# Neighbourhood attention: high and low parts of the probabilities side by side in one product with the values

## The chip, the cores and the metric

The kernel runs on one core of a Trainium2 chip. A core has a matrix engine (TensorE, PE in the profile, with its weight loads as PEld), a vector engine (VectorE, DVE), a scalar engine (ScalarE, ACT), a general engine (GpSimd, POOL) and a queue engine for transfers (SyncE, SP). The metric is the device time of one execution in microseconds; the kernel before takes 2171.08 us, the median of 3 runs (2170.97 to 2171.12).

## The reference

One encoder layer in float32 is applied to two inputs, a sample of 512 tokens and a prompt of 1024 tokens, each of width 1024. Cut to what matters:

```python
z = rmsnorm(x) @ w_in      # q_A k_A v_A | q_B k_B v_B | gate_A gate_B
o_a = attention over all tokens (8 query heads, 2 key heads, rotary)
o_b = neighbourhood_attention(q_B, k_B, v_B, rpb)
x = x + (sigmoid(gate_A) * (o_a @ w_pa) + sigmoid(gate_B) * (o_b @ w_pb)) @ w_out
x = x + relu(rmsnorm(x) @ w_up)**2 @ w_down
y = rmsnorm(x)
```

Neighbourhood attention is what the change touches. Tokens lie on a grid 64 columns wide. A query sees a window of 8 rows by 16 columns around itself; per head (8 heads of 64)

```python
s = einsum('bqhd,bkhd->bhqk', q, k) * scale + bias        # bias by row and column offset
s = where(mask, s, -1e30);  p = softmax(s)
o = einsum('bhqk,bkhd->bqhd', p, v)
```

## The kernel before

**Precision.** Matrix products of float32 quality are made from operands rounded to float32r. A value x is cut into a high part, `hi = round(x)`, written by ScalarE (a copy into a float32r tile), and a low part, `lo = x - hi`, written by VectorE (a subtraction). Most products are then three: hi·hi, hi·lo and lo·hi (`mm3`, L195 to L197).

**Stages.** The work runs in this order: branch A of the sample, branch B of the sample, its projections and output; the same for the prompt; then the MLP of both. In the profile branch B lies at about 190 to 322 us (sample) and 806 to 1090 us (prompt).

**Branch B.** It works in units of one head and one strip of 16 grid columns, 8 x 4 = 32 units per input. A strip has 128 queries in the sample (8 rows) and 256 in the prompt (16 rows, two halves of 128). Each half looks at a rectangle of keys 32 columns wide: 256 keys in the sample, 384 in the prompt. A unit has three steps, each lagging a unit or two behind the one before:

- `s_unit`: scores on TensorE (L933, tiles sbs), bias and row maximum on VectorE (L936), exponential and row sum on ScalarE (L941), reciprocal on VectorE (L943), scaling on GpSimd (L944, tile pbs).
- `t_unit`: the probabilities are transposed by TensorE in blocks of 128 x 128 (L956, tiles ptbs in PSUM); ScalarE writes the high parts (L961, tile bhs), VectorE the low parts (L962, tile bls). The two tiles are laid out as (128 keys) x (key block) x (half) x (128 queries).
- `v_unit`: products with the values into one PSUM bank (L977, tile obs). The values of a key block, tile vss, are the stationary operand, 128 keys x 128 columns: 64 columns of high parts and 64 columns of low parts. The moving operand is the high tile, then the low tile, of the same key block, accumulated into the same bank. The sample has two key blocks, each 128 queries wide: four products of 128 columns. The prompt has four key blocks, of which two are seen by both halves (256 columns) and two by one half (128 columns): four products of 256 columns and four of 128.

The output bank then holds, on partitions 0 to 63, p·v_hi and, on partitions 64 to 127, p·v_lo, for p = p_hi + p_lo. `finish_o` adds them: ScalarE copies the upper half to a tile ot (L430), VectorE adds the lower half to it into a tile os (L439, or L434 for the last two heads). For the first six heads os goes to DRAM (tensor obd) by a transfer issued from ScalarE's queue (L440); for the last two heads it is cut into high and low parts on the chip (L435, L436; tile oXs). Branch A uses the same `finish_o` with 512 queries (tiles os, ot_As, os_As).

**What fills TensorE meanwhile.** While a unit's softmax runs on the other engines, TensorE works off products that belong to no unit: the gate's (tiles gpss), and towards the end the projection of branch A (tiles ppas). They are generators of which a set number of steps is pulled between the steps of a unit. The queries and keys of the next pair of heads are also projected in between, once every eight units (tiles pqbs, pkbs; evacuated at L877 to L903).

**Buffers.** Gate, projection, transposes and outputs of branch B take turns in one pool of four PSUM banks (`mm`); scores have a pool of their own. Tile ot has one buffer, os two, bhs and bls two each.

**Order.** Each engine works off its own queue strictly in order. The order in a queue is set by the framework's planner, which starts from the program's order and moves instructions by estimated times, except where the program pins them (`keep_in_program_order`, not used here). Waits between engines are semaphores set by the framework from what reads and writes which tile.

Of the kernel before, what the change touches and what calls it, by code (L numbers as in the profile page):

```python
# [12 lines left out]
F32R = mybir.dt.float32r  # L13
BF16 = mybir.dt.bfloat16
AF = mybir.ActivationFunctionType
ALU = mybir.AluOpType
AX = mybir.AxisListType

P = 128
D = 1024  # L20
NC8 = D // P
HD = 64
# [39 lines left out]
def encoder(ctx: ExitStack, tc: tile.TileContext, xs, outs, w):  # L62
    nc = tc.nc
# [23 lines left out]
    def slot(shape, dt, name, left=False):  # L87
        return (s8l if left else s8r).tile(shape, dt, tag="s8", name=name)
# [4 lines left out]
    def mm(name):  # L93
        return pmm.tile([P, 512], F32, tag="mm", name=name)
# [295 lines left out]
    def run(tr, nxt, first):  # L390
        N, x, T, NT, NB = tr.N, tr.x, tr.T, tr.NT, tr.NB
        xh, xl = tr.xh, tr.xl
        rows = T // GRID_W
        halves = rows // 8
# [32 lines left out]
        def finish_o(o, n, dst, pool, nm, parts=None):  # L427

            t = pool.tile([HD, 512], F32, tag="ot", name=f"ot_{nm}", bufs=1)
            nc.scalar.activation(t[:, :n], o[HD:P, :n], AF.Copy)  # L430
            if parts is not None:
                hi, lo, ps = parts
                b = pool.tile([P, 512], F32, tag="os", name=f"os_{nm}", bufs=2)[ps, :n]
                nc.vector.tensor_tensor(b, o[0:HD, :n], t[:, :n], op=ALU.add)  # L434
                nc.scalar.activation(hi, b, AF.Copy)  # L435
                nc.vector.tensor_tensor(lo, b, hi.bitcast(F32), op=ALU.subtract)  # L436
                return
            b = pool.tile([HD, 512], F32, tag="os", name=f"os_{nm}", bufs=2)
            nc.vector.tensor_tensor(b[:, :n], o[0:HD, :n], t[:, :n], op=ALU.add)  # L439
            nc.scalar.dma_start(dst, b[:, :n])  # L440
# [43 lines left out]
        for g in range(2):  # L484
            with phase(f"phR{N}_{g}") as ph:
# [143 lines left out]
                for tt in range(NT):  # L629
                    tb, j = divmod(tt, 4)  # L630
                    nm = f"{N}_{g}_{tt}"
# [13 lines left out]
                    op = nc.sync.dma_start(rt, w["rope"][tt * P : (tt + 1) * P])  # L645
# [46 lines left out]
            with phase(f"phA{N}_{g}") as ph:  # L692
# [25 lines left out]
                def pv(u, kc, hi, lo):  # L718
                    h, qb = u
                    if kc == 0:  # L720
                        o_of[u] = mm(f"o{N}_{g}_{h}_{qb}")
                    o = o_of[u]
                    nc.tensor.matmul(o, vhl[:, kc, :], hi, start=(kc == 0), stop=False)
                    nc.tensor.matmul(o, vhl[:, kc, :], lo, start=False, stop=(kc == NT - 1))
                    if kc == NT - 1:
                        r0 = (g * 4 + h) * HD
                        finish_o(o, 512, oad[r0 : r0 + HD, qb * 512 : qb * 512 + 512], ph, f"A{N}_{g}_{h}_{qb}")
# [6 lines left out]
                for ui, u in enumerate(units):  # L734
                    h, qb = u
# [8 lines left out]
                    for kc in range(NT):  # L744
# [5 lines left out]
                        hi = ph.tile([P, 512], F32R, tag="pth", name=f"pth{N}_{g}_{h}_{qb}_{kc}", bufs=3)  # L750
                        lo = ph.tile([P, 512], F32R, tag="ptl", name=f"ptl{N}_{g}_{h}_{qb}_{kc}", bufs=3)
# [69 lines left out]
        nkc = kr_n // 4  # L821
        nkey = kr_n * 32
        nq = rows * 16
        with phase(f"phB{N}") as ph:
            msk = ph.tile([P, halves * 3, nkey], BF16, tag="msk", name=f"msk{N}", bufs=1)
            nc.gpsimd.dma_start(msk, w["mask2"] if halves == 2 else w["mask1"])
            rects, strips, bms, PT = {}, {}, {}, {}
# [120 lines left out]
            def t_unit(u):  # L948
                h, j = u
                nm = f"{N}_{h}_{j}"  # L950
                pt = [mm(f"ptb{nm}_{hf}") for hf in range(halves)]
                hi = ph.tile([P, rows // 4, halves, P], F32R, tag="bh", name=f"bh{nm}", bufs=2)
                lo = ph.tile([P, rows // 4, halves, P], F32R, tag="bl", name=f"bl{nm}", bufs=2)
                for hf in range(halves):
                    for i in range(nkc):
                        nc.tensor.transpose(  # L956
                            pt[hf][:, i * P : (i + 1) * P], PT[u][hf][:, i * P : (i + 1) * P], ident
                        )
                    src = pt[hf][:, : nkc * P].rearrange("p (k q) -> p k q", q=P)
                    dh, dl = hi[:, hf : hf + nkc, hf, :], lo[:, hf : hf + nkc, hf, :]  # L960
                    nc.scalar.activation(dh, src, AF.Copy)  # L961
                    nc.vector.tensor_tensor(dl, src, dh.bitcast(F32), op=ALU.subtract)  # L962
                PT[u] = (hi, lo)

            def v_unit(u):
                h, j = u
                nm = f"{N}_{h}_{j}"
                hi, lo = PT.pop(u)
                o = mm(f"ob{nm}")
                if halves == 2:  # L970
                    seq = [(1, 0, 2), (2, 0, 2), (0, 0, 1), (3, 1, 2)]
                else:
                    seq = [(0, 0, 1), (1, 0, 1)]
                n = 0
                for kc, a, b in seq:
                    for part in (hi, lo):
                        nc.tensor.matmul(  # L977
                            o[:, a * P : b * P],
                            strips[h][:, j, kc, :],
                            part[:, kc, a:b, :],  # L980
                            start=(n == 0),
                            stop=(n == 2 * len(seq) - 1),
                            skip_group_check=True,
                        )
                        n += 1
                if h < 6:
                    finish_o(o, nq, obd[h * HD : h * HD + HD, j * nq : (j + 1) * nq], ph, f"B{nm}")
                else:
                    if not oX3:
                        oX3.append(slot([P, 2, T], F32R, f"oX{N}_1_3"))  # L990
                    ps = slice(64 * (h % 2), 64 * (h % 2) + 64)
                    hi, lo = (oX3[0][ps, i, j * nq : (j + 1) * nq] for i in range(2))
                    finish_o(o, nq, None, ph, f"B{nm}", (hi, lo, ps))
# [8 lines left out]
            n = len(units)  # L1002
# [3 lines left out]
            for i in range(n + LS + LV):  # L1006
                if i < n - 8:
                    f = (5 if i < LS else 2 + i % 2) if NB == 1 else 5 + (i % 3 > 0)
                else:
                    f = 3 + i % 2 if NB == 1 else 7  # L1010
# [16 lines left out]
                if 0 <= i - LS < n:  # L1027
                    t_unit(units[i - LS])
# [16 lines left out]
                if 0 <= i - LS - LV < n:  # L1045
                    v_unit(units[i - LS - LV])
# [4 lines left out]
        with phase(f"phG{N}") as ph:  # L1051
# [25 lines left out]
            for c in range(NC8):  # L1077
# [3 lines left out]
                for tb in range(NB):  # L1081
# [4 lines left out]
                    nm = f"{N}_{c}_{tb}"  # L1086
# [11 lines left out]
                    hi, lo = (mgs[tb, c // 4][i][:, c % 4, :] for i in range(2))  # L1098
# [18 lines left out]
            for half in range(2):  # L1117
                wo = wos[half]
                hc = slice(half * 512, half * 512 + 512)
                for tt in range(NT):  # L1120
                    tb, j = divmod(tt, 4)
                    nm = f"{N}_{half}_{tt}"
# [17 lines left out]
                    if half == 0 and NB == 1:  # L1140
# [4 lines left out]
                        o = o4[tt]  # L1145
                    else:
                        o = mm(f"op{nm}")
# [27 lines left out]
                    if half == 1:  # L1175
# [8 lines left out]
                        else:  # L1184
# [10 lines left out]
                            if 3 <= tt <= 5:  # L1195
                                j = tt - 3
# [560 lines left out]
```

## Time and profile before

| | us |
|---|---|
| median of the runs (lowest, highest) | 2171.08 (2170.97, 2171.12) |
| the profiled execution | 2169.37 |
| its span, first to last instruction | 2167.6 |
| TensorE, products busy | 2129.6 |
| VectorE busy | 1449.2 |
| ScalarE busy | 1104.6 |
| GpSimd busy | 364.6 |

Busy time is the time in which at least one instruction of the engine is under way. Products on TensorE are pipelined, so the duration of one runs into the next; the distance between two starts is what one of them takes of the queue. A group's row names line, engine and operation, output <- inputs by the program's names, the shapes, the count, then busy time, mean time of one in ns, and the idle time of the engine before them with what ended it. A row of time names the start, the duration, engine, line and operation, with idle time ahead of it in brackets. In rows, "f32" stands for float32r operands too.

### The profile page before, as it was taken

The numbers are of one execution on the slowest core, as the hardware profiler recorded it, in microseconds if no ns is written. First come the engines' busy times: TensorE is split into PE (matmuls) and PEld (weight loads), VectorE is DVE, ScalarE is ACT, GpSimd is POOL, SyncE is SP. The second block draws the span as 40 slices with busy tenths as digits, with TensorE's granted clock in tenths as the row PEclk, the third lists the DMA queues.
The fourth block names the chain that finished last, engine by engine and source line by source line (L and its number), as shares of the span: only waits on it lengthen the run. The fifth ranks groups of instructions, "written<-read, shape, count | busy, mean of one in ns | idle before, by whom it ended". The sixth has DMA issues, their size and how long they took to land. (4 is left out here: it accounts for less than half of the span.)

```text
span 2167.6 us, 32386 instructions
## 1 busy us (share of the span) xinstructions
PE 2129.6 (98%) x11159; PEld 1864.2 (86%) x11159; DVE 1449.2 (67%) x2825; ACT 1104.6 (51%) x2367; POOL 364.6 (17%) x470
## 2 busy tenths in 40 slices
PE   8999999899999999999999999999999999999998
PEld 8887788788898888888888899998999988888886
DVE  6665666777757754545782777778777777769563
ACT  5654653656645744545530565666555543434352
POOL 2232210332233313323200200003000000000000
PEclk9999999999999999999999999999999999999999
DMA  6437447620122133433463656668445799788561
GB/s 190 125 108 216 125 140 253 203 75 23 48 76 82 45 90 101 135 106 103 142 205 126 205 175 195 193 220 220 157 153 165 234 349 340 222 273 282 173 201 62
DMA packets 321259, 354.09 MB, mean 163 GB/s; under 512 B 31551, under 2 KB 255431, under 8 KB 321095
## 3 DMA queue, kind: packets, MB, share of 16 engines
q1 hardware_dynamic: 277927, 279.65, 41.5%
q10 hardware_dynamic: 36016, 52.19, 6.9%
q0 software_dynamic: 7152, 20.19, 3.5%
q8 instruction: 88, 1.44, 0.3%
q14 instruction: 76, 0.62, 0.1%
HBM read 264.85 MB, written 87.88 MB: 163 GB/s over the span
## 5 line engine op out<-in xcount | busy, mean ns | idle before, releaser
L197 PE MATMUL dn<-wd,al 128*128 128x512 f32 x624 | 242.8, 389 | 0.0
L196 PE MATMUL dn<-wd,ah 128*128 128x512 f32 x624 | 242.8, 389 | 0.0
L195 PE MATMUL dn<-wd,ah 128*128 128x512 f32 x624 | 242.7, 389 | 0.0
L1234 ACT ACTIVATE ah<-ar 128x512 fp32r<-128x512 f32 x168 | 104.2, 628 | 200.2 <-PE dn L196 186.1
L1235 DVE TENSOR_TENSOR al<-ar,ah 128x512 fp32r<-128x512 f32 x168 | 114.9, 692 | 73.9 <-ACT ah L1234 64.5
L197 PEld LDWEIGHTS dn<-wd,al 128*128 128x128 f32 x624 | 117.1, 188 | 24.4
L195 PEld LDWEIGHTS dn<-wd,ah 128*128 128x128 f32 x624 | 117.1, 188 | 24.3
L196 PEld LDWEIGHTS dn<-wd,ah 128*128 128x128 f32 x624 | 117.1, 188 | 24.2
L753 DVE TENSOR_TENSOR ptls<-pTs,pths 128x512 fp32r<-128x512 f32 x160 | 107.7, 686 | 39.1 <-ACT pths L752 38.6
L713 POOL TENSOR_SCALAR ps<-ps,rls 128x1024 f32<-128x1024 f32 (+1 forms) x96 | 96.9, 1010 | 213.5 <-DVE rls L712 197.6
L752 ACT ACTIVATE pths<-pTs 128x512 fp32r<-128x512 f32 x160 | 94.2, 598 | 74.0 <-PE pTs L747 71.8
L707 DVE TENSOR_REDUCE nms<-ss 128x1 f32<-128x1024 f32 (+1 forms) x96 | 99.9, 1041 | 25.4 <-PE ss L705 25.0
L195 PE MATMUL gpss<-xs_0h,w_gs 128*128 128x512 f32 x256 | 105.6, 412 | 0.5 <-DVE bls L962 0.5
L710 ACT ACTIVATE ps<-ss,nms 128x1024 f32<-128x1024 f32 (+1 forms) x96 | 93.3, 972 | 22.6 <-DVE nms L707 20.0
L180 POOL TENSOR_TENSOR rs_f<-ms_f,mhalf 128x1 f32<-128x1 f32 x6 | 4.0, 668 | 590.7 <-DVE ms_f L176 590.7
L747 PEld LDWEIGHTS pTs<-ident,ps 128*128 128x128 f32 x640 | 78.1, 140 | 28.3 <-POOL ps L713 4.1
L196 PE MATMUL gpss<-xs_0l,w_gs 128*128 128x512 f32 x256 | 101.0, 394 | 0.0
L197 PE MATMUL gpss<-xs_0h,w_gs 128*128 128x512 f32 x256 | 100.7, 393 | 0.0
L747 PE MATMUL pTs<-ident,ps 128*128 128x128 f32 x640 | 98.9, 274 | 1.3 <-DVE ptls L753 0.6
L1234 ACT ACTIVATE A<-S 128x512 fp32r<-128x512 f32 x128 | 75.8, 623 | 30.3 <-DVE S L1297 23.0
L919 POOL TENSOR_TENSOR bms<-rects,msks 128x384 f32<-128x384 f32 (+1 forms) x72 | 64.7, 901 | 150.1 <-DVE nmbs L936 124.1
L195 PE MATMUL ud<-B,A 128*128 128x384 f32 x256 | 85.7, 335 | 1.5 <-DVE c L1352 1.5
(328 smaller groups left out, 6417.7 us busy)
## 6 DMA issues: line engine op xcount, KB each, us to landing
ar<-ud SPq DMA_DIRECT2D x120, 512.0 KB
br<-in_w_mlp_down_dram SPq DMA_DIRECT2D x72, 512.0 KB
rawu<-in_w_mlp_up_dram SPq DMA_DIRECT2D x64, 512.0 KB
ud<-c ACTq DMA_DIRECT2D x128, 192.0 KB
raw_gs<-in_w_in_dram SPq DMA_DIRECT2D x32, 512.0 KB
zgs<-sgs ACTq DMA_DIRECT2D x48, 256.0 KB
ud<-cs SPq DMA_DIRECT2D x64, 192.0 KB
raw_os<-in_w_out_dram SPq DMA_DIRECT2D x16, 512.0 KB
```

The source lines that it names most:

```text
L195: nc.tensor.matmul(out, ah, bh, start=start, stop=False, **kw)
L196: nc.tensor.matmul(out, ah, bl, start=False, stop=False, **kw)
L197: nc.tensor.matmul(out, al, bh, start=False, stop=stop, **kw)
L707: nc.vector.tensor_reduce(nm_, s, axis=AX.X, op=ALU.max, negate=True)
L710: nc.scalar.activation(p, s, AF.Exp, bias=nm_, accum_out=l)
L713: nc.gpsimd.tensor_scalar(p, p, rl, 1.0, op0=ALU.mult, op1=ALU.mult)
L747: nc.tensor.transpose(pt[:, j * P : (j + 1) * P], PP[u, j][:, kc * P : (kc + 1) * P], ident)
L752: nc.scalar.activation(hi, pt, AF.Copy)
L753: nc.vector.tensor_tensor(lo, pt, hi.bitcast(F32), op=ALU.subtract)
L919: nc.gpsimd.tensor_tensor(bm.rearrange("p (r c) -> p r c", c=32), rects[h][:, ir : ir + kr_n, jr : jr + 32], msk[:, hf * 3 + ct, :].rearra ...
L1234: nc.scalar.activation(hi, src, AF.Copy)
L1235: nc.vector.tensor_tensor(lo, src, hi.bitcast(F32), op=ALU.subtract)
```

## The change

The high and low parts of a unit's probabilities go into one tile, side by side for each key block: (128 keys) x (key block) x (high, low) x (half) x (128 queries). One product per key block then takes both parts as its moving operand, and high and low results go to different columns of the bank: columns 0 to n are p_hi·v, columns n to 2n p_lo·v. The sample has two products of 256 columns per unit, the prompt two of 512 and two of 256. `finish_o` now gets an output with three dimensions: ScalarE copies the upper 64 partitions of both column ranges into ot, VectorE adds the lower 64 partitions of both in place (a new instruction), and the old addition then adds the two column ranges. Branch A's outputs take the old path.

```diff
         def finish_o(o, n, dst, pool, nm, parts=None):
             t = pool.tile([HD, 512], F32, tag="ot", name=f"ot_{nm}", bufs=1)
-            nc.scalar.activation(t[:, :n], o[HD:P, :n], AF.Copy)
+            if len(o.shape) == 3:
+                tv = t[:, : 2 * n].rearrange("p (i q) -> p i q", i=2)
+                nc.scalar.activation(tv, o[HD:P], AF.Copy)
+                nc.vector.tensor_tensor(tv, o[0:HD], tv, op=ALU.add)
+                o = tv[:, 1]
+            else:
+                nc.scalar.activation(t[:, :n], o[HD:P, :n], AF.Copy)
...
             def t_unit(u):
...
-                hi = ph.tile([P, rows // 4, halves, P], F32R, tag="bh", name=f"bh{nm}", bufs=2)
-                lo = ph.tile([P, rows // 4, halves, P], F32R, tag="bl", name=f"bl{nm}", bufs=2)
+                hl = ph.tile([P, rows // 4, 2, halves, P], F32R, tag="bh", name=f"bh{nm}", bufs=2)
...
-                    dh, dl = hi[:, hf : hf + nkc, hf, :], lo[:, hf : hf + nkc, hf, :]
+                    dh, dl = (hl[:, hf : hf + nkc, i, hf, :] for i in range(2))
                     nc.scalar.activation(dh, src, AF.Copy)
                     nc.vector.tensor_tensor(dl, src, dh.bitcast(F32), op=ALU.subtract)
-                PT[u] = (hi, lo)
+                PT[u] = hl

             def v_unit(u):
...
-                o = mm(f"ob{nm}")
+                o = mm(f"ob{nm}")[:, : 2 * nq].rearrange("p (i q) -> p i q", i=2)
                 if halves == 2:
                     seq = [(1, 0, 2), (2, 0, 2), (0, 0, 1), (3, 1, 2)]
                 else:
                     seq = [(0, 0, 1), (1, 0, 1)]
-                n = 0
-                for kc, a, b in seq:
-                    for part in (hi, lo):
-                        nc.tensor.matmul(
-                            o[:, a * P : b * P],
-                            strips[h][:, j, kc, :],
-                            part[:, kc, a:b, :],
-                            start=(n == 0),
-                            stop=(n == 2 * len(seq) - 1),
-                            skip_group_check=True,
-                        )
-                        n += 1
+                for n, (kc, a, b) in enumerate(seq):
+                    nc.tensor.matmul(
+                        o[:, :, a * P : b * P],
+                        strips[h][:, j, kc, :],
+                        hl[:, kc, :, a:b, :].rearrange("p i a q -> p i (a q)"),
+                        start=(n == 0),
+                        stop=(n == len(seq) - 1),
+                        skip_group_check=True,
+                    )
```

More of the change, by code (lines that the diff above doesn't have):

```diff
@@ L967, in v_unit @@
                 nm = f"{N}_{h}_{j}"
-                hi, lo = PT.pop(u)
-                o = mm(f"ob{nm}")
+                hl = PT.pop(u)
+                o = mm(f"ob{nm}")[:, : 2 * nq].rearrange("p (i q) -> p i q", i=2)
                 if halves == 2:
```

## The prediction

> **What bounds the kernel now.** I read the page's totals, then the two stretches in which branch B runs (the sample, 512 tokens, at 190 to 322 us; the prompt, 1024 tokens, at 806 to 1090 us), then TensorE's instructions in order of time, then what TensorE waited for.
>
> The page, span and totals:
>
> ```profile
> span 2167.6 us, 32386 instructions
> PE 2129.6 (98%) x11159; PEld 1864.2 (86%) x11159; DVE 1449.2 (67%) x2825; ACT 1104.6 (51%) x2367; POOL 364.6 (17%) x470
> ```
>
> Busy time by stretch, the two of branch B first, then the two crowded slices of ten microseconds:
>
> ```profile
> core 0: us, PE busy (x) PEld busy (x) DVE busy (x) ACT busy (x) POOL busy (x), PEclk, DMA share, GB/s
> 190.00:322.00 132.00, 128.38 (x679) 106.72 (x679) 82.93 (x266) 75.55 (x188) 36.16 (x56) 1.00 0.50 147
> 806.00:1090.00 284.00, 281.37 (x1463) 235.18 (x1462) 158.04 (x441) 138.25 (x309) 87.77 (x115) 1.00 0.39 116
> 260.00:270.00 10.00, 9.57 (x55) 8.04 (x56) 8.66 (x29) 7.31 (x18) 5.51 (x7) 1.00 0.36 99
> ...
> 1020.00:1030.00 10.00, 9.06 (x47) 7.07 (x46) 9.76 (x22) 6.68 (x16) 3.74 (x4) 1.00 0.30 74
> ```
>
> TensorE is idle for 132 - 128.4 = 3.6 us of the sample's stretch and 284 - 281.4 = 2.6 us of the prompt's, at the full clock (PEclk 1.00). VectorE has 49 and 126 us free, though not everywhere: 8.66 of 10 us in one slice, 9.76 in another. What TensorE waited for, the sample's stretch and then the prompt's (who waits <- for whom, us in total, times, longest):
>
> ```profile
> PE obs L977 <- ACT sgs L423: 1.8, 1, 1.8
> PE sbs L933 <- DVE kBs L899: 0.5, 1, 0.5
> PE gpss L195 <- DVE bls L962: 0.5, 1, 0.5
> PE obs L977 <- DVE os_Bs L439: 0.4, 1, 0.4
> PE ptbs L956 <- ACT sgs L423: 0.3, 1, 0.3
> ```
>
> ```profile
> PE sbs L933 <- DVE nmbs L936: 0.9, 2, 0.6
> PE sbs L933 <- DVE kBs L899: 0.8, 1, 0.8
> PE gpss L195 <- DVE bls L962: 0.4, 1, 0.4
> PE obs L977 <- DVE bls L962: 0.3, 1, 0.3
> ```
>
> So TensorE's own queue sets the end of both stretches, and a product taken from it is worth its slot.
>
> **The slots.** A duration of a product (0.27 us and more) overlaps the next one; what counts is the distance from start to start. TensorE in order of time, one unit of the sample and one of the prompt:
>
> ```profile
> 304.56 0.39 PE L196 MATMUL ppas<-oXs,w_pas 128*128 128x512 f32 x1
> 304.79 0.39 PE L197 MATMUL ppas<-oXs,w_pas 128*128 128x512 f32 x1
> 305.02 0.22 PE L977 MATMUL obs<-bhs,vss 128*128 128x128 f32 x1
> 305.07 0.28 PE L977 MATMUL obs<-bls,vss 128*128 128x128 f32 x1
> 305.19 0.27 PE L977 MATMUL obs<-bhs,vss 128*128 128x128 f32 x1
> 305.30 0.27 PE L977 MATMUL obs<-bls,vss 128*128 128x128 f32 x1
> 305.41 0.45 PE L933 MATMUL sbs<-kBs,qBs 128*128 128x256 f32 x2
> ```
>
> ```profile
> 953.18 0.28 PE L977 MATMUL obs<-bhs,vss 128*128 128x256 f32 x1
> 953.30 0.28 PE L977 MATMUL obs<-bls,vss 128*128 128x256 f32 x1
> ...
> 953.66 0.22 PE L977 MATMUL obs<-bhs,vss 128*128 128x128 f32 x1
> ...
> 954.05 0.57 PE L933 MATMUL sbs<-kBs,qBs 128*128 128x384 f32 x2
> ```
>
> A product 512 wide takes a slot of 0.23 us (304.56, 304.79, 305.02), one 256 wide 0.12 (953.18 to 953.30), and 128 wide 0.11 (305.07, 305.19, 305.30): half the width saves almost nothing, so the narrow ones are the ones that joining removes.
>
> **The change part by part.**
>
> *Products, L977.* The changed program issues 192 products where the old one has 384: per unit of the sample two of 256 in place of four of 128, per unit of the prompt two of 512 and two of 256 in place of four of 256 and four of 128. Sample: 305.41 - 305.02 = 0.39 us becomes 2 x 0.12 = 0.24, so 0.15 saved, times 32 units = 4.8 us. Prompt: 954.05 - 953.18 = 0.87 becomes 2 x 0.23 + 2 x 0.12 = 0.70, so 0.17, times 32 = 5.4 us. Together 10.2 us, all on TensorE's queue. What the new operand could add: it is read in two pieces of 128 or 256 columns, and no row shows a product over pieces; the 384-wide score products just behind (953 row, two in 0.57 us) read keys in pieces of 32 columns, so I put no extra on it.
>
> The Trainium skill, "TensorE: Matmul & The Clock Gate", section "LDWEIGHTS (loading the stationary operand)", gives 128 / 1.2 = 107 ns for a weight load; the trace agrees, the 128-wide slots being 0.11 us. Its section "Back-to-back issue gap" gives N / 2.4 + 2.5 ns for a wide product, 216 and 109 ns here, by which (an estimate) the sum would be 32 x (0.39 - 0.218) + 32 x (0.87 - 0.65) = 12.5 us instead of 10.2; the trace is slower than that at 0.23 and 0.12. The same section's 81 ns for 128 columns and 131 ns for 512 in a stream is not what this trace shows.
>
> *Evacuation.* ScalarE copies twice the width, VectorE gets one more addition, twice as wide and straight from PSUM, and the old addition stays (its operands both in SBUF now). Groups by shape:
>
> ```profile
> L430 ACT ACTIVATE ot_Bs<-obs 64x256 f32<-64x256 f32 x32 | 12.2, 382 | 58.5 <-PE obs L977 58.3
> L439 DVE TENSOR_TENSOR os_As<-os,ot_As 64x512 f32<-64x512 f32 x16 | 10.9, 682 | 7.4 <-ACT ot_As L430 7.4
> L439 DVE TENSOR_TENSOR os_Bs<-obs,ot_Bs 64x256 f32<-64x256 f32 x24 | 9.9, 412 | 0.1
> L430 ACT ACTIVATE ot_As<-os 64x512 f32<-64x512 f32 x16 | 9.5, 595 | 5.7 <-PE os L724 5.7
> L430 ACT ACTIVATE ot_Bs<-obs 64x128 f32<-64x128 f32 x32 | 8.8, 274 | 8.6 <-PE obs L977 5.4 <-DVE bls L962 1.1 <-PE ptbs L956 0.5
> L439 DVE TENSOR_TENSOR os_Bs<-obs,ot_Bs 64x128 f32<-64x128 f32 x24 | 6.7, 279 | 0.8 <-ACT ot_Bs L430 0.6
> ```
>
> VectorE: 32 x 0.41 = 13.2 us in the sample, 32 x 0.68 = 21.8 us in the prompt, 35 us in all. ScalarE: 32 x (0.38 - 0.27) = 3.5 and 32 x (0.60 - 0.38) = 7 us. The cover is the free time above. VectorE's load goes from 82.9 / 132 = 63% to 96.1 / 127 = 76%, and from 56% to 179.8 / 279 = 64%. It is a queue that TensorE now and then waits for, so I let the waits put down to it grow as load / (1 - load): from 1.69 to 3.1 (sample, 1.4 us of waits become 2.6) and from 1.26 to 1.8 (prompt, 2.4 become 3.5). ScalarE's 2.1 us in the sample, load 57% to 62%, become 2.6. Together 2.8 us given back. What is queued behind the wide addition on VectorE: the score pass L936, the reciprocal L943 and the low parts L962, which lead to the transposes L956 and the next products.
>
> *Bounds of that term.* Below: the waits do not grow, 0; nothing shows a gain, except that fewer products could also shorten a wait, at most the 6.2 us now waited. Above: every VectorE addition lands on TensorE's path, 35 us. I take 2.8, near the lower end, because the waits that TensorE shows now are 6.2 us under 241 us of VectorE work.
>
> *The bank.* The output bank, one of four that rotate, comes free after the wider copy and the wide addition: (0.38 - 0.27) + (0.41 - 0.28) = 0.24 us later in the sample, 0.22 + 0.27 = 0.49 in the prompt. In the rows above one wait of 0.4 us is for that release (obs <- os_Bs), in the sample. I leave this inside the 2.8.
>
> *One buffer for both parts.* The first product now also waits for the low part, which before only the second did: 0.06 to 0.12 us at a unit where the low part ends last. One such wait stands above (obs <- bls, 0.3 us). Nothing.
>
> *The store's issue* sits on ScalarE's queue and waits for the last addition, now one operation later; exponentials and high-part copies stand behind it. 48 issues as before, none moved past another queue. Inside the ScalarE term. *End of a stretch:* the last unit's result is needed by the fourth contraction step of branch B's projection; nine products of 0.23 us stand ahead of it, 2 us against a chain that is under 1 us longer. Nothing. *Order:* the planner's order of TensorE is the old one but for score products and transposes shifted by a few places; on VectorE weight splits and reciprocals change places around the new addition. Unknown sign, put into the range.
>
> **Sum.** -10.2 + 2.8 = -7.4 us. The profiled execution took 2169.4 us (span 2167.6), 1.7 us under the median 2171.1; against the median the forecast is 2171.1 - 7.4 = 2163.7 us, -0.34%. A measurement of this kernel tells changes from about 0.2%, 4.3 us.
>
> **Rivals.**
>
> *Full gain.* Waits do not grow, or shrink, and slots come out a little shorter: -10.2 to -13, 2158 to 2161 us. For it: five waits of under a microsecond in the prompt's rows, VectorE at 56%. Against: slices like 1020 to 1030, where VectorE is full and TensorE already loses 0.94 of 10 us.
>
> *VectorE takes the sample's gain back.* In the sample the units stand three to four microseconds apart, and in slices at 8.66 of 10 the new 0.41 us per unit fills VectorE. If 13.2 us are exposed by a half to all, the sample goes from -4.8 to between +2 and +8, the prompt stays near -4: net -2 to +4, 2169 to 2175 us, no change to be told. For it: the two crowded slices. Against: 49 us free in the stretch. The Trainium skill, "Perfetto Trace Analysis", section "Identifying the Most-Contended Engine", says that matmul busy time is a bad measure of TensorE's headroom and that weight-load busy time is a better one; by it (81% and 83% in the stretches' rows) TensorE would have room and the shorter products would be worth less, ending here, about 2171 us. The trace speaks against that: the slots follow one another at 0.23 and 0.11 us without a gap.
>
> *Slower: the held bank.* If each next user of the four-bank ring already waits when the output bank comes free, its later release goes onto TensorE whole: 32 x 0.24 + 32 x 0.49 = 23.4 us, net +13, 2184 us. It turns the sign when 10.2 / 23.4 = 44% of the units are caught, and passes +0.2% at 62%. Against: now one unit of 64 is caught.
>
> **How the numbers follow.** Forecast (2161 to 2167) 0.53, full gain 0.18, VectorE 0.17, the held bank 0.12. Faster by over 0.2%: 0.53 + 0.18 + a part of VectorE's lower end, 0.04 = 0.75; within: 0.11 of VectorE's; slower: 0.12 + 0.02 = 0.14. Range 2158 to 2172: full gain, forecast and the lower half of VectorE's case.
>
> **What would show it.** After: 192 products of L977's successor at slots of 0.12 and 0.23 us; both stretches shorter, by some 3 and 4 us; 64 new VectorE additions of 0.41 and 0.68 us; VectorE near 76% and 64% there; TensorE's idle time in the stretches 8 to 10 us in place of 6.2. Wrong if a wide product in two pieces takes more than 0.27 us, if waits on the new addition by itself pass 5 us, or if the rest of the kernel moves by more than 2 us.

## The result and the profile after

The changed kernel takes 2157.32 us (median of 6 runs, 2155.98 to 2159.72) against 2171.09 us before (median of 6); the ratio is 0.9939, 95% interval 0.9926 to 0.9951, that is 13.2 us less (10.6 to 16.1). The forecast was 2163.7 with a range from 2158 to 2172: the direction was right, the gain came out almost twice as large, just outside the range.

The page of the changed kernel, span and totals:

```profile
span 2154.6 us, 32045 instructions
PE 2116.6 (98%) x10967; PEld 1847.1 (86%) x10967; DVE 1480.2 (69%) x2889; ACT 1113.2 (52%) x2367; POOL 370.4 (17%) x470
```

The span is 13.0 us shorter, with 192 products fewer and 64 VectorE instructions more. To compare the two stretches of branch B, I cut both kernels at the same work: from the first score product to the first product of branch B's projection. Busy time by stretch, before:

```profile
188.50:321.60 133.10, 129.48 (x683) 107.41 (x683) 84.19 (x267) 75.27 (x187) 36.16 (x56) 1.00 0.51 149
811.30:1089.00 277.70, 275.07 (x1436) 230.23 (x1435) 155.34 (x433) 135.96 (x304) 87.77 (x115) 1.00 0.40 116
```

and after:

```profile
core 0: us, PE busy (x) PEld busy (x) DVE busy (x) ACT busy (x) POOL busy (x), PEclk, DMA share, GB/s
187.10:315.20 128.10, 124.16 (x619) 101.14 (x619) 95.57 (x298) 77.23 (x186) 38.38 (x56) 1.00 0.54 155
805.80:1075.50 269.70, 267.93 (x1307) 220.30 (x1307) 172.81 (x464) 143.00 (x304) 91.51 (x115) 1.00 0.42 122
```

The sample's stretch is 5.0 us shorter, the prompt's 8.0. That the span is shorter by the same 13.0 us is partly chance: what lies between the stretches and behind the second is 1.0 and 0.5 us longer, and what lies ahead of the first, which the change does not touch, is 1.4 us shorter. The latter goes with TensorE's granted clock (PEclk), here in the same five microseconds before and after:

```profile
175.00:180.00 5.00, 5.00 (x15) 3.98 (x16) 3.46 (x5) 2.00 (x2) 1.21 (x1) 0.66 1.08 342
175.00:180.00 5.00, 4.91 (x22) 4.08 (x23) 3.62 (x6) 2.01 (x2) 1.20 (x1) 1.00 1.10 345
```

A second profile of the changed kernel (the repeat, further down) has 0.66 there too. Its sample's stretch starts at 188.2 us instead of 187.1, its span is 2155.7 us, and its two stretches take 128.3 and 269.7 us.

VectorE stands at 95.6 / 128.1 = 75% and 172.8 / 269.7 = 64%, as forecast. TensorE's idle time is 3.9 + 1.8 = 5.7 us, where it was 3.6 + 2.6 = 6.2: it did not rise.

TensorE in order of time, a unit of the sample and one of the prompt, after:

```profile
296.25 0.39 PE L197 MATMUL ppas<-oXs,w_pas 128*128 128x512 f32 x1
296.48 0.40 PE L982 MATMUL obs<-bhs,vss 128*128 128x256 f32 x2
296.72 0.40 PE L940 MATMUL sbs<-kBs,qBs 128*128 128x256 f32 x2
296.96 0.40 PE L195 MATMUL ppas<-oXs,w_pas 128*128 128x512 f32 x1
```

```profile
944.19 0.86 PE L982 MATMUL obs<-bhs,vss 128*128 128x512 f32 x4
944.88 0.52 PE L940 MATMUL sbs<-kBs,qBs 128*128 128x384 f32 x2
945.24 0.40 PE L195 MATMUL gpss<-xs_1h,w_gs 128*128 128x512 f32 x1
```

The groups take 0.24 and 0.69 us, as forecast (0.24 and 0.70). But the pair of score products behind them takes 0.24 and 0.36 us. Before, in the units that the prediction showed, that pair ran from 305.41 and from 954.05 to these rows:

```profile
305.70 0.40 PE L195 MATMUL ppas<-oXs,w_pas 128*128 128x512 f32 x1
...
954.46 0.40 PE L195 MATMUL gpss<-xs_1h,w_gs 128*128 128x512 f32 x1
```

that is 0.29 and 0.41 us. The pair, which the change does not touch, got 0.05 us shorter in each.

What TensorE waited for after, in the sample and in the prompt:

```profile
PE obs L982 <- DVE bhs L969: 1.1, 1, 1.1
PE pqbs L195 <- ACT sgs L423: 0.8, 1, 0.8
PE gpss L195 <- DVE ot_Bs L434: 0.5, 1, 0.5
PE sbs L940 <- ACT kBs L904: 0.5, 1, 0.5
PE ptbs L963 <- ACT sgs L423: 0.4, 1, 0.4
PE obs L982 <- ACT sgs L423: 0.3, 1, 0.3
PE ptbs L963 <- DVE rlbs L950: 0.2, 1, 0.2
```

```profile
PE sbs L940 <- DVE kBs L906: 0.8, 1, 0.8
PE gpss L195 <- DVE bhs L969: 0.4, 1, 0.4
PE sbs L940 <- DVE nmbs L943: 0.2, 1, 0.2
PE obs L982 <- issue: 0.2, 1, 0.2
```

One wait of 0.5 us is for the new wide addition (ot_Bs L434), that is for the held bank; the longest, 1.1 us, is for a low part (obs <- bhs L969). The wide additions cost what was forecast, by the groups of the changed kernel:

```profile
L434 DVE TENSOR_TENSOR ot_Bs<-obs,ot_Bs 64x512 f32<-64x512 f32 x32 | 21.8, 680 | 4.1 <-ACT ot_Bs L433 3.9
...
L434 DVE TENSOR_TENSOR ot_Bs<-obs,ot_Bs 64x256 f32<-64x256 f32 x32 | 13.2, 412 | 1.7 <-ACT ot_Bs L433 1.3
```

Open at this point: is the surplus in the products, or did the evacuation cost nothing?

### The profile page after: what moved, and what is told of

Read it like the earlier page. It is cut to its first block, busy times and chain, and to the rows that moved or that the text cites. A ratio compares the mean times of both kernels' runs of the same rounds, so it can differ in the third digit from the quotient of the medians.

```text
span 2154.6 us, 32045 instructions
## 1 busy us (share of the span) xinstructions
PE 2116.6 (98%) x10967; PEld 1847.1 (86%) x10967; DVE 1480.2 (69%) x2889; ACT 1113.2 (52%) x2367; POOL 370.4 (17%) x470
## 5 line engine op out<-in xcount | busy, mean ns | idle before, releaser
L926 POOL TENSOR_TENSOR bms<-rects,msks 128x384 f32<-128x384 f32 (+1 forms) x72 | 71.2, 991 | 130.1 <-DVE nmbs L943 108.7
L1239 DVE TENSOR_TENSOR A<-S,A 128x512 fp32r<-128x512 f32 x128 | 84.5, 686 | 4.2 <-ACT A L1238 4.1
```

The costliest lines, as they stand in the source:

```text
L926: nc.gpsimd.tensor_tensor(bm.rearrange("p (r c) -> p r c", c=32), rects[h][:, ir : ir + kr_n, jr : jr + 32], msk[:, hf * 3 + ct, :].rearra ...
L1239: nc.vector.tensor_tensor(lo, src, hi.bitcast(F32), op=ALU.subtract)
```

## The experiments

Ratios are against the kernel before on the same chip, with 95% intervals; it took 2169.7 to 2170.0 us there.

### The products alone, and the evacuation alone

The products alone: wide products, but only the high part's columns are evacuated, in the old way (the low part's product is left out of the result).

```diff
                         skip_group_check=True,
                     )
+                o = o[:, 0]
```

> The wide products of the changed kernel, but only the columns of the high part are evacuated, by the old narrow copy and the one old addition; the low part's product is left out of the result. Before is 2171.1 us, the changed kernel 2157.3. Theory P (as predicted: the slots are worth 10.2 us, the wider evacuation gives 2.8 back): 2160.9, above the changed kernel, which P cannot explain. Theory Q (the slots with the score product behind them are worth 6.4 + 7.4 = 13.8 us and the evacuation is covered): 2157.3, the same as the changed kernel within 1.5. Theory R (the products are worth more still and the evacuation gives back the 2.8 of the prediction): 2154.5.

Measured: 2154.84 us, ratio 0.9933 (0.9920 to 0.9945), 14.5 us less. Busy time by stretch:

```profile
188.24:314.11 125.87, 123.73 (x620) 101.09 (x620) 85.00 (x267) 74.85 (x187) 37.24 (x56) 1.00 0.55 160
803.78:1073.54 269.76, 267.72 (x1308) 220.31 (x1308) 154.70 (x433) 136.24 (x304) 86.12 (x115) 1.00 0.42 121
```

The evacuation alone: the narrow products of before, but out of the joined tile, and high and low parts go to columns of their own, and the wide evacuation follows.

```diff
-                for n, (kc, a, b) in enumerate(seq):
-                    nc.tensor.matmul(
-                        o[:, :, a * P : b * P],
...
-                        hl[:, kc, :, a:b, :].rearrange("p i a q -> p i (a q)"),
...
+                for kc, a, b in seq:
+                    for i in range(2):
+                        nc.tensor.matmul(
+                            o[:, i, a * P : b * P],
...
+                            hl[:, kc, i, a:b, :],
```

> The narrow products of before (384 of them), writing high and low parts to their own columns, with the wide evacuation of the changed kernel: 32 x 0.41 + 32 x 0.68 = 35 us more on VectorE, 10 us more on ScalarE, nothing gained on TensorE. Theory P and R: 2171.1 + 2.8 = 2173.9 or more. Theory Q (covered): 2171.1, at most 0.7 more. The bank rival: up to 2194.5.

Measured: 2171.97 us, ratio 1.0011 (1.0002 to 1.0020), 0.4 to 4.3 us more.

```profile
188.42:322.63 134.21, 129.49 (x680) 107.03 (x680) 95.40 (x295) 78.02 (x186) 37.64 (x56) 1.00 0.51 147
813.51:1091.20 277.69, 275.41 (x1436) 230.21 (x1435) 173.55 (x464) 143.01 (x304) 88.83 (x115) 1.00 0.41 119
```

So the products are worth more than the 10.2 us of the prediction, and the evacuation does cost a little. In the prompt it costs nothing: 277.69 us with narrow products and 269.76 or 269.70 with wide ones, whichever way the bank is emptied. In the sample it costs: 134.2 against 133.1 us with narrow products (from which the joined tile is not separated), 128.1 against 125.9 with wide ones. In spans, 2152.1 for the products alone and 2154.6 for the whole change, it is 2.5 us. Against the repeat's span of 2155.7, in which the sample's stretch starts at 188.2 us as in that of the products alone, it is 3.6.

### One input at a time

The wide products and the wide evacuation for the sample alone, then for the prompt alone; the other input keeps the narrow products and the old evacuation, out of the joined tile.

```diff
+                if halves == 1:          # halves == 2 in the second kernel
+                    (wide products as in the changed kernel)
+                else:
+                    (narrow products as before, part taken from hl[:, kc, i, a:b, :])
```

> Wide products and wide evacuation for the sample (512 tokens) alone, the prompt as before but for the joined tile. Theory P: 4.8 gained, 1.7 given back, 2168.0. Theory Q: 32 x 0.20 = 6.4 gained, 2164.7; if VectorE's crowded slices in the sample cost something, between the two.

> Wide products and wide evacuation for the prompt (1024 tokens) alone, the sample as before but for the joined tile. Theory P: 5.4 gained, 1.1 given back, 2166.8. Theory Q: 32 x 0.23 = 7.4 gained, 2163.7. The two halves of the change should add up to 13.8 if nothing outside the stretches moves.

Measured: sample alone 2165.65 us, ratio 0.9981 (0.9972 to 0.9989), 4.1 us less; prompt alone 2163.29 us, ratio 0.9967 (0.9954 to 0.9979), 7.2 us less. Together 11.3 us, against 13.2 for the whole change, within the intervals. The prompt's 7.2 us (4.6 to 10.0) fit the slots counted with the score pair (7.4); the sample's 4.1 (2.4 to 6.1) fall between that theory (6.4) and the prediction (3.1). The stretches say it more closely. The sample alone, then the prompt alone, with five microseconds of the latter's sample between its two rows:

```profile
188.29:316.54 128.25, 124.16 (x620) 101.14 (x620) 95.68 (x298) 77.12 (x186) 38.21 (x56) 1.00 0.54 156
807.08:1084.47 277.39, 274.93 (x1435) 230.25 (x1435) 155.20 (x433) 135.85 (x304) 87.50 (x115) 1.00 0.40 119
```

```profile
188.43:323.88 135.45, 130.87 (x684) 108.91 (x683) 84.49 (x267) 75.50 (x187) 35.48 (x56) 0.99 0.51 148
225.00:230.00 5.00, 5.00 (x22) 4.23 (x22) 3.88 (x12) 4.00 (x9) 1.82 (x3) 0.66 0.52 146
813.51:1082.79 269.28, 267.70 (x1308) 220.36 (x1307) 173.66 (x464) 143.01 (x304) 90.90 (x115) 1.00 0.42 122
```

The sample's stretch is 4.9 us shorter with its own part of the change, the prompt's 8.4, against 5.0 and 8.0 with both: the two parts add up. Left with narrow products and the old evacuation, the prompt's stretch takes 277.4 us, as before (277.7), so the joined tile by itself costs nothing there. For the sample this cannot be read: its 135.4 us hold a fall of the granted clock to 0.66 in 225 to 230 us, and a wait for the gate of 2.7 us where 1.8 stood before.

### Who pays for a narrow product

In the kernel before, the prompt's narrow products are moved inside the group, so that a 256-wide pair comes last.

```diff
-                    seq = [(1, 0, 2), (2, 0, 2), (0, 0, 1), (3, 1, 2)]
+                    seq = [(1, 0, 2), (0, 0, 1), (3, 1, 2), (2, 0, 2)]
```

> The kernel before, with the prompt's narrow products (128 columns) moved inside the group, so that a 256-wide pair comes last, ahead of the score products. Before: 0.87 us for the group and 0.41 for the pair of score products behind it; changed kernel: 0.69 and 0.36. If any product behind a narrow one pays for it, the group and the pair take 1.28 us together as before and the time is that of before. If only the score products pay, 1.23 us and 1.6 us less in all.

Measured: 2170.26 us, ratio 0.9999 (0.9990 to 1.0008). TensorE in order of time, from one group:

```profile
954.10 0.28 PE L977 MATMUL obs<-bhs,vss 128*128 128x256 f32 x1
...
954.34 0.22 PE L977 MATMUL obs<-bhs,vss 128*128 128x128 f32 x1
954.40 0.27 PE L977 MATMUL obs<-bls,vss 128*128 128x128 f32 x1
...
954.62 0.28 PE L977 MATMUL obs<-bls,vss 128*128 128x128 f32 x1
954.73 0.33 PE L977 MATMUL obs<-bhs,vss 128*128 128x256 f32 x1
954.90 0.28 PE L977 MATMUL obs<-bls,vss 128*128 128x256 f32 x1
955.02 0.52 PE L933 MATMUL sbs<-kBs,qBs 128*128 128x384 f32 x2
955.38 0.40 PE L195 MATMUL gpss<-xs_1h,w_gs 128*128 128x512 f32 x1
```

The 256-wide product behind the last narrow one now takes 0.17 us (954.73 to 954.90), the next one 0.12, and the score pair 0.36. Group and pair take 955.38 - 954.10 = 1.28 us, as in the kernel before. Over all units of the prompt, the groups take 29.7 us instead of 28.1 and the pairs 25.8 instead of 27.4. So the 0.05 us is a part of the narrow product's price that its follower shows, whatever the follower is. The first narrow product, behind a wide one, shows as much less: 0.06 us from its start to the next (954.34 to 954.40), where the later ones take 0.11. The price of 0.11 us each is there, but the end of it appears one start later.

### More VectorE work in the evacuation

The wide addition is issued twice, so that the lower half of the bank goes into the result twice.

```diff
                 nc.vector.tensor_tensor(tv, o[0:HD], tv, op=ALU.add)
+                nc.vector.tensor_tensor(tv, o[0:HD], tv, op=ALU.add)
```

> The changed kernel with the new wide addition issued twice (the lower half of the bank is added twice, so the result is not the attention's). 35 us more on VectorE on its queue, and the bank is held 0.41 or 0.68 us longer. The prediction's way of growing waits (load / (1 - load), VectorE from 75% to 85% in the sample and from 64% to 72% in the prompt) gives about 3 us more, 3 of them in the sample. If the evacuation is covered: as the changed kernel within 1. If VectorE is at its limit in the sample already: up to 13 us more there, nothing in the prompt, whose stretch came out at 269.7 us with and without the wide evacuation.

Measured: 2164.20 us, ratio 0.9972 (0.9962 to 0.9982): 6.1 us less than before, so about 7 us of the change's gain are gone. By stretch, and what the first products of branch B's projection waited for behind the sample's:

```profile
188.33:318.42 130.09, 125.32 (x620) 101.24 (x619) 101.38 (x320) 75.99 (x184) 39.72 (x56) 1.00 0.50 144
812.12:1083.88 271.76, 269.04 (x1307) 220.39 (x1307) 193.63 (x494) 143.77 (x304) 86.93 (x115) 1.00 0.42 121
```

```profile
PE ppbs L196 <- DVE oXs L190: 1.2, 2, 0.8
PE ppbs L195 <- ACT oXs L443: 1.1, 1, 1.1
```

The first 35 us of VectorE work (with 10 us of ScalarE's) cost 2.5 us, the second 35 us about 7: the cover is there, and it wears out. The growth rule of the prediction gave 3 for this step. Two of the us are lost in each stretch (128.1 to 130.1 and 269.7 to 271.8), and 3 between them (493.7 us where it was 490.6): the projection behind the sample now waits for the results of the last units, 2.3 us in three waits, where the changed kernel shows no such wait.

### Shorter evacuations

Three versions take work off VectorE. First, the last addition goes to GpSimd:

```diff
+            eng = nc.gpsimd if len(o.shape) == 3 else nc.vector
...
-            nc.vector.tensor_tensor(b[:, :n], o[0:HD, :n], t[:, :n], op=ALU.add)
+            eng.tensor_tensor(b[:, :n], o[0:HD, :n], t[:, :n], op=ALU.add)
```

> The changed kernel with the last addition of the two column ranges (both operands in SBUF) on GpSimd in place of VectorE: VectorE gets 32 x 0.28 + 32 x 0.41 = 22 us of work less, GpSimd that much and more. The sample's stretch was 125.9 us with the narrow evacuation and 128.1 with the wide one; if that 2.2 us is VectorE's queue, most of it comes back, 2 us under the changed kernel. If it is the longer chain behind the bank or the order, nothing comes back; GpSimd's own queue (30% busy in the sample, with the scaling of the probabilities behind the addition) can make it slower by 1 to 3.

Measured: 2161.89 us, ratio 0.9958 (0.9944 to 0.9972). It is slower than the change by some 3 to 4 us (ratio 0.9958; the changed kernel has 0.9939 and, repeated, 0.9945; the intervals overlap a little). The stretches agree: 130.1 and 270.9 us, 2.0 and 1.2 longer than the change's. Two groups of this kernel:

```profile
L949 ACT ACTIVATE pbs<-sbss,nmbs 128x384 f32<-128x384 f32 x64 | 39.3, 615 | 39.4 <-POOL os_Bs L447 19.9 <-DVE nmbs L944 16.7 <-DVE mAs L822 1.5
...
L447 POOL TENSOR_TENSOR os_Bs<-ot_Bs 64x256 f32<-64x256 f32 x24 | 18.8, 783 | 12.1 <-DVE ot_Bs L435 9.4 <-DVE rlbs L951 2.7
```

The addition takes 0.78 us on GpSimd, where the same 24 additions took 0.45 each on VectorE. The store of its result is issued from ScalarE's queue, and 19.9 us of idle time ahead of the exponentials behind it end with GpSimd; the idle time of that row is 39.4 us, in the changed kernel it was 30.0, so it grew by 9.4. TensorE is idle for 9.0 us of the two stretches, where it was 5.7. The load is off VectorE, and the chain behind the bank is longer; the chain weighs more. Whether it is the store's wait that does it, or GpSimd's queue with the scaling of the probabilities behind the addition, is not shown.

Second, GpSimd folds the copied upper half over the two column ranges, and VectorE makes two narrow additions:

```diff
-                nc.vector.tensor_tensor(tv, o[0:HD], tv, op=ALU.add)
-                o = tv[:, 1]
+                nc.gpsimd.tensor_tensor(tv[:, 0], tv[:, 0], tv[:, 1], op=ALU.add)
+                nc.vector.tensor_tensor(t[:, :n], o[0:HD, 0], t[:, :n], op=ALU.add)
+                o = o[:, 1]
```

> The changed kernel with the copied upper half folded over the two column ranges on GpSimd, and two narrow additions on VectorE in place of the wide and the narrow one: 32 x 0.13 + 32 x 0.27 = 13 us less on VectorE, but one more hand-over before the bank comes free. If VectorE's queue is the 2.2 us in the sample: 1 us under the changed kernel. If the chain is: 1 to 3 us above it.

Measured: 2163.59 us, ratio 0.9968 (0.9957 to 0.9980), again slower than the change, by some 5 to 6 us (the stretches take 131.8 and 272.2 us). The edit adds one more hand-over before the bank comes free: VectorE's first addition stands behind 34 us of idle time that end with the fold on GpSimd (20.1 in the prompt, 13.9 in the sample). Whether that alone is the cause is not shown.

Third, nothing on GpSimd, and less to do: the product of the two low parts is left out, so that the low columns need only their lower half.

```diff
-                nc.scalar.activation(tv, o[HD:P], AF.Copy)
-                nc.vector.tensor_tensor(tv, o[0:HD], tv, op=ALU.add)
-                o = tv[:, 1]
+                nc.scalar.activation(t[:, :n], o[HD:P, 0], AF.Copy)
+                nc.vector.tensor_tensor(t[:, :n], o[0:HD, 0], t[:, :n], op=ALU.add)
+                o = o[:, 1]
```

> The wide products with a narrower evacuation: ScalarE copies the upper half of the high columns alone (the product of the two low parts is left out, as it is everywhere else in this kernel), VectorE adds the lower half of the high columns and then the lower half of the low columns, two narrow additions of 0.28 (sample) or 0.41 us (prompt) in place of 0.41 + 0.28 and 0.68 + 0.41. Against before VectorE gets 22 us more instead of 35, ScalarE nothing. If the evacuation's price in the sample is VectorE's and ScalarE's load, the time lies between the products alone (ratio 0.9933) and the changed kernel (0.9939), about 2 us under the changed kernel of the same call at best; if it is the chain that holds the bank, as the changed kernel.

> The changed kernel as it is, beside the one with the narrower evacuation: ratio 0.9939 as before, within 0.9926 to 0.9951.

Measured side by side: 2154.86 us (2154.66 to 2155.27), ratio 0.9930 (0.9917 to 0.9944), beside 2157.81 us (2157.46 to 2159.25), ratio 0.9945 (0.9932 to 0.9957), for the changed kernel again. The runs of the two do not overlap: 3 us under the change, 15 us under the kernel before, and as fast as the products alone.

```profile
188.19:314.40 126.21, 123.95 (x619) 100.60 (x619) 91.71 (x298) 73.77 (x186) 38.45 (x56) 1.00 0.54 155
804.03:1074.32 270.29, 268.03 (x1307) 220.23 (x1307) 169.72 (x464) 136.42 (x304) 86.35 (x115) 1.00 0.42 122
```

VectorE still has 91.7 us of work in the sample (95.6 with the wide evacuation, 85.0 with the old one), and the sample's stretch is at 126.2 us from first score product to first projection product, close to the 125.9 of the products alone. The prompt's stretch gains nothing; it is 0.6 us longer than the repeat's. In the sample the bank is held no shorter than with the wide evacuation, a copy and two additions of 0.27 + 0.28 + 0.28 us against 0.38 + 0.41, so the hold is not what was saved. Whether it was VectorE's work (7 us less than in the repeat, over both stretches), ScalarE's (10 us less) or the shorter way to the store is not shown.

## Why the prediction was right and wrong

**What bounds the kernel: right.** TensorE's queue sets the end of both stretches. Taking products out shortened the stretches by what they and their followers took, and by some waits besides. Adding 35 us of VectorE work to the narrow products cost 0.4 to 4.3 us.

**The step that failed: both terms of the sum, "Products" at -10.2 us and the waits at +2.8.** The following sums are over all units, from the rows of time, start to start and without TensorE's idle time. The groups go from 13.6 to 8.3 us in the sample and from 28.1 to 22.4 in the prompt, 11.0 us less; the score products go from 9.8 to 9.5 and from 27.4 to 26.0, 1.7 us less; TensorE's idle time goes from 6.2 to 5.7, 0.5 us less. So -12.7 stands where the prediction had -10.2, and -0.5 where it had +2.8. Together they are 13.2 us; the two stretches are 13.0 us shorter. In the kernel with the products alone the three are 11.2, 2.2 and 2.1 us, 15.5 in all, and its stretches are 15.2 us shorter.

*Products.* The prediction priced the groups from one row each: 0.39 us in the sample, where the mean of the 32 is 13.6 / 32 = 0.43. Means in place of single rows, before and after, make 0.8 of the 2.5 us that this term lacked. The other 1.7 are the follower's. The prediction read the 128-wide slot as 0.11 us from three starts (305.07, 305.19, 305.30) and passed over the one ahead of them, 305.02 to 305.07: the first narrow product shows only 0.05 us, and the score pair behind the last shows the rest. It ended its count at the pair's start, and so left out 0.05 us for each such pair; the moved products show that the narrow product ahead is what causes it. In the prompt this is 1.4 us over all units. In the sample it is only 0.3, where other products than the score pair now stand behind some of the groups.

*Waits.* The prediction let them only grow, from the 6.2 us of the kernel before; that fewer products could shorten one it put into its bounds and not into the sum. With the products alone they fell to 4.2 us, and the evacuation brought them back to 5.7. Why they fell, no run settles: they are a handful of single waits, and other ones in each kernel.

**The given-back 2.8 us: near in size, by luck.** The evacuation by itself costs 2.5 or 3.6 us in spans, by the profile that is taken, and 2.6 between the short evacuation and the repeated change (2153.1 and 2155.7). It is not where the rule of load put it. It costs nothing in the prompt. In the sample it is 2.3 us, 1.8 of them TensorE idle time (2.1 to 3.9). Another 0.9 us lie between the stretches, which are 489.6 us apart in every kernel whose sample is evacuated in the old or the short way, and 490.4 to 490.9 in those with the wide copy; the kernel with the addition twice has 493.7. Product by product against the short evacuation, most of the 0.9 us is lost at one place in the prompt's branch A, where TensorE waits 0.64 us in the repeat (at 487.75 us, the transpose pTs for ptls) and not at all with the short evacuation; why there, is open. Doubling the addition cost twice what the rule gave.

**The slots of the new products: right** (0.24 and 0.69 us), and no price for reading the operand in two pieces. The Trainium skill, "TensorE: Matmul & The Clock Gate", section "LDWEIGHTS (loading the stationary operand)", gives 128 / 1.2 = 107 ns for loading 128 columns of weights. The trace agrees in the sum: four narrow products with what their follower shows take 0.39 + 0.05 = 0.44 us, 0.11 each.

**The rivals.** "Full gain" had the right side, and was right that the waits do not grow. The slots did not come out shorter, as it had supposed, and its bound of -13 us was too near, for want of the followers. "VectorE takes the sample's gain back" did not come: the sample alone is 4.1 us faster. But it is one more such operation away: with the doubled addition the way from the sample's first score product to the prompt's takes 623.8 us, before 622.8. The held bank did not come: one wait of 0.5 us on the wide addition. **End of a stretch** cost nothing in the changed kernel, but did with the doubled addition, 2.3 us of waits. **One buffer for both parts** cost nothing in the prompt (277.4 us with the joined tile alone); in the sample one wait of 1.1 us on the low part (obs <- bhs) stands where the list before had none, the 0.3 us having been the prompt's. **The store's issue** may well be on the path that matters: when the last addition moved to GpSimd, the exponentials behind the store stood idle 9.4 us longer; that this is what slowed the kernel was not shown by itself.

## What to carry to other kernels

Count a group of products from its first start to the start behind its follower, and take the mean over all units: here products of 128 columns cost 0.11 us each, almost as much as products of 256 (0.12), and a part of that shows at the one behind them. So joining two narrow products that share their stationary operand saves almost one of them; joining products of 256 columns to 512 saves next to nothing (four at 0.12 us against two at 0.23). When results land in more columns, ask which corners are needed at all before adding engines: leaving one out was worth 3 us, moving the addition to a less busy engine lost 3 to 4.

Compare profiles by stretches that hold the same work, and mind the granted clock ahead of them: of the 13.0 us between the two spans, 1.4 lay there.

## What was not expected of the hardware

A wide product behind a 128-wide one takes 0.17 us instead of 0.12 (256 columns), a score pair 0.41 instead of 0.36; a 128-wide one behind a wide one takes 0.06 instead of 0.11. Waits of TensorE became fewer when its own products did, 6.2 to 4.2 us (one profile of each). An addition over 64 partitions by 256 columns, both operands in SBUF, takes 0.78 us on GpSimd and 0.45 on VectorE. TensorE's granted clock was 0.66 in 175 to 180 us of one profile of the changed kernel and 1.00 there in the other, and the work behind started about 1 us later in the first.
